# The mLSTM branch of a hybrid encoder block on one core: earlier row loads, one copy out of PSUM, the head norm in SBUF

## The chip, the core and the metric

The kernel runs on one core of a Trainium2 chip. The metric is the device time of one execution, in microseconds (us). The engines that run at the same time are PE (TensorE, matrix products), DVE (VectorE), ACT (ScalarE), POOL (GpSimd) and SP (SyncE, which here only issues DMA transfers). Each engine works its own queue in order; semaphores tie the queues together. PSUM is the memory that PE writes its products to, in banks of 512 columns; SBUF is the memory of everything else on the core.

## What is computed

One layer of a streaming encoder on 1024 tokens of width 1024: half a SwiGLU block, one projection into all the columns that a sparse attention and an mLSTM need, these two branches, their gated merge, and another half SwiGLU block. The change touches only the mLSTM branch. In the reference its scan over chunks is:

```python
D = b[..., :, None] - b[..., None, :] + ic[..., None, :]
...
W = jnp.einsum('bhtd,bhsd->bhts', qc, kc) * jnp.exp(D - m_t[..., None])
w_int = jnp.exp(inter - m_t)
num = jnp.einsum('bhts,bhsv->bhtv', W, vc) + w_int[..., None] * jnp.einsum('bhtd,bhdv->bhtv', qc, C)
den = jnp.sum(W, axis=-1) + w_int * jnp.einsum('bhtd,bhd->bht', qc, n)
h = num / jnp.maximum(jnp.abs(den), jnp.exp(-m_t))[..., None]
...
C_new = wc[..., None, None] * C + jnp.einsum('bhs,bhsd,bhsv->bhdv', ws, kc, vc)
...
h = rms_norm(h, head_g.reshape(H, MLSTM_V_DIM))
```

There are 4 heads of 64 key and 128 value columns. All of it is float32.

## The kernel before

The chip's work in this stretch is the input projection (called mixing here): each product of a 128-column block of weights is made of three float32 passes over halves of split weights, at lines 795, 796 and 797. `pump` (line 1305) advances that projection by one step, a tick, of six matmuls of 128x512, and at each tick also runs what is due: `later(n, f)` puts a function n ticks ahead, and `turn_later(n, src, then)` does the same with four PE transposes in front. ACT line 534 and POOL line 535 split each weight tile into a rounded part and its rest (`round<-raw`) ahead of the matmuls that use it. Results of the projection leave their banks through ACT lines 1230 and 1239 and DVE lines 1232, 1266 and 1271. At the same time the top-k search of the sparse attention runs in the background: counts on DVE (lines 1610 to 1617) and on ACT (lines 1640 to 1642).

`mlstm` (line 1808) handles the 1024 tokens in 8 chunks of 128 (t = 0 to 7), spread over 62 ticks, so 7.75 ticks to a chunk: half of them before the chunk's output products and half behind.

- `load(t)` fetches q, k and v of a chunk, two chunks ahead.
- `begin(t)` transposes k (line 1843) and forms k·q for the four heads (line 1846) in PSUM, and then loads two rows of 512 numbers, each broadcast to 128 partitions (line 1854): d_m into E and d_w into qw. ACT takes the exponential of E, head by head (line 1857); POOL cuts E to the causal triangle (line 1859); DVE multiplies E by k·q (line 1863) and qw by q (line 1864).
- The chunk's output is made at lines 1877 and 1878: for each head 129 columns, 128 of the numerator and one of the denominator, in banks 4 and 5 (`out`). The state is advanced by lines 1883 (PE) and 1886 (DVE).
- Then comes the head norm: DVE copies the denominators out of PSUM (line 1894) and makes reciprocals (1895 to 1897); ACT squares the four heads straight out of PSUM with row sums (line 1900); DVE line 801 and POOL line 802 take the inverse root of the means; DVE line 1903 joins both factors and line 1904 multiplies the numerators, reading PSUM. Only when line 1904 is done may the next chunk's line 1877 write banks 4 and 5.
- Seven ticks after the chunk's second half the result is transposed (line 1349), copied by ACT (line 1914) and stored to d_h (line 1915).

What order these instructions take on each engine is set by the framework's scheduler, which plans all of them by a cost model; `issue_after` puts an instruction behind another that is named. SBUF buffers are drawn from pools whose tiles the traces name extra, more, spare, plain and rawx; a DMA into a reused tile waits until its last user is done.

Of the kernel before, what the change touches and what calls it, by code (L numbers as in the profile page):

```python
# [22 lines left out]
AF = mybir.ActivationFunctionType  # L23
ALU = mybir.AluOpType
# [4 lines left out]
P = 128  # L29
# [679 lines left out]
class Block:  # L709
# [1098 lines left out]
    def mlstm(self, upto):  # L1808

        nc, ar = self.nc, self.ar  # L1810
# [15 lines left out]
        four = lambda ap: ap.rearrange("p (x e) -> p x e", x=2)  # L1826
# [10 lines left out]
        def begin(t):  # L1837
# [10 lines left out]
            kws, E, qw = ar.alloc(256), ar.alloc(512), ar.alloc(512)  # L1848
# [4 lines left out]
            for dst, src in ((E, self.d_m), (qw, self.d_w)):  # L1853
                nc.sync.dma_start(dst.f, src[t:t + 1, :].partition_broadcast(P)[:, 0, :])
# [14 lines left out]
        now = begin(0)  # L1869
        for t in range(8):  # L1870
            self.pump(halves / 8 * 0.5)
# [21 lines left out]
            den, ss = sm[t % 2].f[:, 0:4], sm[t % 2].f[:, 4:8]  # L1893
            v.tensor_copy(four(ss), out[:, :, :, 128])
            v.scalar_tensor_tensor(den, ss, -1.0, ss, ALU.mult, ALU.max)
            v.tensor_tensor(den, den, self.floor[:, t * 4:t * 4 + 4], ALU.max)
            v.reciprocal(den, den)
            nd = ar.alloc(512)
            for h in range(4):
                nc.scalar.activation(nd.f[:, h * P:(h + 1) * P], out[:, h // 2, h % 2, 0:128], AF.Square,  # L1900
                                     scale=den[:, h:h + 1], accum_out=ss[:, h:h + 1])
            self.rsqrt_mean(ss, 128, 4)
            v.tensor_tensor(den, den, ss, ALU.mult)
            v.tensor_tensor(nd.f.rearrange("p (x e c) -> p x e c", x=2, e=2), out[:, :, :, 0:128],
                            four(den)[:, :, :, None].to_broadcast([P, 2, 2, P]), ALU.mult)
            if t < 7:
                now = begin(t + 1)
            self.pump(halves / 8 * 0.5)


            def store(ps, nd=nd, t=t):
                nd.free()
                s = ar.alloc(512)
                nc.scalar.activation(s.f, ps, AF.Copy)
                nc.sync.dma_start(self.d_h[:, :, t * P:(t + 1) * P].rearrange("h p c -> p h c"),
                                  s.f.rearrange("p (h c) -> p h c", h=4))
                s.free()
# [544 lines left out]
```

## Time and profile before

| | us |
|---|---|
| median of 3 runs (lowest to highest) | 2093.31 (2091.74 to 2093.69) |
| the profiled execution | 2092.13 |
| its span in the trace | 2090.4 |
| mLSTM chunks in the trace | about 900 to 1090 |

The profiled execution lies 1.2 us under the median. Its mean granted TensorE clock is 0.997 of full speed. In a row of the timeline, what stands in brackets is the time that the engine had been idle before that instruction and what ended the idle time. Start times count from the start of the span.

### The profile page before, as it was taken

To read this page: it belongs to the slowest core of one execution; us is meant where nothing else is said; L and a number is where in the kernel's file an instruction comes from. 1 tells how busy PE (TensorE), PEld (TensorE's weight loads), DVE (VectorE), ACT (ScalarE), POOL (GpSimd) and SP (SyncE) were. 2 spreads that over 40 slices of the span, in tenths; PEclk is the share of its full clock that TensorE was granted. 3 is DMA by queue.
4 is the path that set the end of the run, shared out by engine and by line. 5 is a ranking of instruction groups with operands and counts; after the bars stand their busy time and mean duration, and the time that the engine had idled before them with its cause. 6 is when DMAs were issued, how large, how long until landed. Compare 5 with 4: busy or idle time off the path is not lost.

```text
span 2090.4 us, 27895 instructions
## 1 busy us (share of the span) xinstructions
PE 2031.9 (97%) x9341; PEld 1667.7 (80%) x9341; DVE 1615.8 (77%) x2815; ACT 1047.4 (50%) x1961; POOL 348.7 (17%) x385
## 2 busy tenths in 40 slices
PE   7999999999999989999998999999999999999999
PEld 6788888888887777787886788788888888888887
DVE  7988887678856676997899589798976676669863
ACT  8332333334436566985786478636533333334442
POOL 1000000000004223443545445312000000000000
PEclk9999999999999999999999999999999999999999
DMA  5498894494634263465665911832333333386331
GB/s 187 142 286 269 279 291 157 136 359 139 210 144 142 63 184 101 107 188 177 183 207 189 332 61 61 293 121 97 126 121 101 111 100 102 110 294 246 126 111 41
DMA packets 289677, 349.85 MB, mean 167 GB/s; under 512 B 21901, under 2 KB 187389, under 8 KB 289405
## 3 DMA queue, kind: packets, MB, share of 16 engines
q1 hardware_dynamic: 289532, 348.07, 51.1%
q8 instruction: 73, 1.20, 0.2%
q14 instruction: 72, 0.58, 0.1%
HBM read 237.34 MB, written 110.66 MB: 166 GB/s over the span
## 4 chain that ended last, share of the span: by engine, by line
PE 47%; DVE 7%; DMA 4%; ACT 3%; issue 2%; POOL 1%; SPq 0%; POOLq 0%; DVEq 0%; ACTq 0%
PE psum L795 14%; PE psum L796 14%; PE psum L797 14%; DVE plain L1610 2%; PE psum L2118 1%; PE psum L1499 1%; PE psum L1500 1%; POOL round L535 1%; PE psum L2173 1%; PE psum L2172 1%; DMA raw<-in_w_proj_b_dram 1%; DMA more<-d_m 1%; DMA side<-d_kg 0%; DVE h L925 0%; DVE plain L1529 0%
## 5 line engine op out<-in xcount | busy, mean ns | idle before, releaser
L795 PE MATMUL psum<-h,round 128*128 128x512 f32 x656 | 260.9, 398 | 3.1 <-ACT more L1239 1.5
L796 PE MATMUL psum<-h,round 128*128 128x512 f32 x656 | 258.6, 394 | 1.0 <-DVE h L925 0.8
L797 PE MATMUL psum<-h,round 128*128 128x512 f32 x656 | 258.0, 394 | 0.5 <-DVE round L302 0.3
L535 POOL TENSOR_TENSOR round<-raw,round 128x512 fp32r<-128x512 f32 x104 | 147.6, 1425 | 142.9 <-ACT round L534 109.7
L795 PEld LDWEIGHTS psum<-h,round 128*128 128x128 f32 x656 | 124.0, 189 | 31.0 <-ACT more L1239 1.9
L797 PEld LDWEIGHTS psum<-h,round 128*128 128x128 f32 x656 | 124.0, 189 | 27.4 <-DVE round L302 0.7
L796 PEld LDWEIGHTS psum<-h,round 128*128 128x128 f32 x656 | 124.2, 189 | 27.0 <-DVE h L925 1.5
L795 PE MATMUL psum<-swap,round 128*128 128x512 f32 x328 | 130.3, 398 | 7.9 <-ACT round L534 3.2
L797 PE MATMUL psum<-swap,round 128*128 128x512 f32 x328 | 129.5, 395 | 0.4 <-POOL round L535 0.4
L796 PE MATMUL psum<-swap,round 128*128 128x512 f32 x328 | 129.0, 393 | 0.4 <-DVE swap L952 0.2
L1610 DVE TENSOR_SCALAR_CACHE_REDUCE plain<-plain 128x384 bf16<-128x384 f32 (+1 forms) x124 | 107.7, 868 | 2.3
L301 ACT ACTIVATE round<-plain 128x512 fp32r<-128x512 f32 x79 | 49.6, 632 | 98.9 <-PE psum L796 77.2
L924 ACT ACTIVATE round<-plain 128x512 fp32r<-128x512 f32 x73 | 45.7, 631 | 100.0 <-PE psum L796 92.7
L878 POOL MEMSET raw<- 128x384 f32 x1 | 0.4, 422 | 526.3 <-DVE round L925 526.3
L797 PE MATMUL psum<-h,extra 128*128 128x512 f32 x212 | 82.5, 390 | 1.5 <-POOL extra L535 1.5
L796 PE MATMUL psum<-side 128*128 128x512 f32 x208 | 80.9, 389 | 0.0
L797 PE MATMUL psum<-side 128*128 128x512 f32 x208 | 80.9, 389 | 0.0
L795 PE MATMUL psum<-side 128*128 128x512 f32 x208 | 80.9, 389 | 0.0
L795 PEld LDWEIGHTS psum<-swap,round 128*128 128x128 f32 x328 | 62.0, 189 | 23.3 <-ACT round L534 4.1
L796 PE MATMUL psum<-h,spare 128*128 128x512 f32 x196 | 76.6, 391 | 1.9 <-DVE h L925 1.9
L795 PE MATMUL psum<-h,spare 128*128 128x512 f32 x196 | 76.9, 394 | 0.8 <-ACT h L924 0.4
L534 ACT ACTIVATE round<-raw 128x512 fp32r<-128x512 f32 x107 | 66.3, 624 | 21.8 <-PE psum L796 15.7
(752 smaller groups left out, 5919.9 us busy)
## 6 DMA issues: line engine op xcount, KB each, us to landing
plain<-d_a SPq DMA_DIRECT2D x154, 256.0 KB
d_a<-plain SPq DMA_DIRECT2D x123, 256.0 KB
raw<-in_ffn_w_gate_dram SPq DMA_DIRECT2D x44, 512.0 KB
raw<-d_s SPq DMA_DIRECT2D x72, 256.0 KB
h<-in_ffn_w_down_dram SPq DMA_DIRECT2D x66, 256.0 KB
plain<-in_w_in_dram SPq DMA_DIRECT2D x29, 512.0 KB
d_s<-plain SPq DMA_DIRECT2D x58, 256.0 KB
raw<-in_w_in_dram SPq DMA_DIRECT2D x55, 256.0 KB
```

The source lines that it names most:

```text
L301: k.nc.scalar.activation(hi.r.rearrange("p (k c) -> p k c", k=4), src, AF.Copy)
L534: self.done_A = k.nc.scalar.activation(hi.r, raw.f, AF.Copy).ins
L535: k.nc.gpsimd.tensor_tensor(lo.r, raw.f, hi.f, ALU.subtract)
L795: mm(ps, lhs[0], rhs[0], start=start, stop=False, skip_group_check=more)
L796: mm(ps, lhs[0], rhs[1], start=False, stop=False, skip_group_check=more)
L797: mm(ps, lhs[1], rhs[0], start=False, stop=stop, skip_group_check=more)
L924: self.split_A = self.nc.scalar.activation(hi, src, AF.Copy).ins
L1499: self.nc.tensor.matmul(o, qb, khi.r[:, s * n:s * n + n], start=True, stop=False)
L1500: last = self.nc.tensor.matmul(o, qb, klo.r[:, s * n:s * n + n], start=False, stop=True).ins
L1610: v.tensor_scalar(s.junk[:, :s.width[j]], s.sc[j], one(s.cand, j), one(s.neg, j), ALU.is_ge, ALU.add, accum_out=one(s.cnt, j))
L2118: self.last = nc.tensor.transpose(ps[:, j * P:(j + 1) * P], pr[j].f[:, kt * P:(kt + 1) * P], self.ident).ins
L2172: mm(po, vr[:, kt, g, :], hi.r, start=kt == 0, stop=False)
```

## The change

Three things are done. First, the two row loads (E and qw) leave `begin` and become a function `weights(t)`, called for the next chunk at the top of the loop, ahead of the first half of the ticks; the new chunk's `begin` is handed the two tiles. Second, one ACT copy takes all 516 columns of `out` from PSUM to an SBUF tile `nd`, behind the last weight split that ACT was given; the separate DVE copy of the denominators goes. Third, the head norm reads `nd` in SBUF, in a function `normed` that is put one tick later; its four Squares write one 128-column tile in turn, its multiplication works in place, and its transposes are put seven ticks behind it.

```diff
--- before.py
+++ after.py
@@ -1823,7 +1823,6 @@
         C = [ar.alloc(2 * 129, keep=True) for _ in range(2)]
         v.memset(C[0].f, 0.0)
         out = self.bank(4, 2).rearrange("p (x c) -> p x c", x=2)[:, :, 0:258].rearrange("p x (e c) -> p x e c", e=2)
-        four = lambda ap: ap.rearrange("p (x e) -> p x e", x=2)
 
         def load(t):
             q4 = qs[t % 2].f.rearrange("p (x e c) -> p x e c", x=2, e=2)
@@ -1834,7 +1833,14 @@
                               self.d_k[t].rearrange("x p c -> p x c"))
             nc.sync.dma_start(vs[t % 2].f.rearrange("p (h c) -> p h c", h=4)[:, :, 0:128], self.d_v[t])
 
-        def begin(t):
+        def weights(t):
+
+            E, qw = ar.alloc(512), ar.alloc(512)
+            for dst, src in ((E, self.d_m), (qw, self.d_w)):
+                nc.sync.dma_start(dst.f, src[t:t + 1, :].partition_broadcast(P)[:, 0, :])
+            return E, qw
+
+        def begin(t, E, qw):
 
             q, k = qs[t % 2].f, ks[t % 2].f
 
@@ -1845,13 +1851,11 @@
             for h in range(4):
                 mm(kq[:, h * P:(h + 1) * P], k[:, h // 2 * P:h // 2 * P + P], q[:, h * P:(h + 1) * P],
                    start=True, stop=True)
-            kws, E, qw = ar.alloc(256), ar.alloc(512), ar.alloc(512)
+            kws = ar.alloc(256)
             v.tensor_tensor(kws.f.rearrange("p (h d) -> p h d", h=4),
                             ps[:, 0:256].rearrange("p (h d) -> p h d", h=4),
                             self.ws[:, t * 4:t * 4 + 4, None].to_broadcast([P, 4, 64]), ALU.mult)
 
-            for dst, src in ((E, self.d_m), (qw, self.d_w)):
-                nc.sync.dma_start(dst.f, src[t:t + 1, :].partition_broadcast(P)[:, 0, :])
             for h in range(4):
                 r = t * 4 + h
                 nc.scalar.activation(E.f[:, h * P:(h + 1) * P], E.f[:, h * P:(h + 1) * P], AF.Exp,
@@ -1866,8 +1870,9 @@
 
         load(0)
         load(1)
-        now = begin(0)
+        now = begin(0, *weights(0))
         for t in range(8):
+            ahead = weights(t + 1) if t < 7 else None
             self.pump(halves / 8 * 0.5)
             kws, E, qw = now
             v1 = vs[t % 2].f.rearrange("p (h c) -> p h c", h=4)
@@ -1890,33 +1895,43 @@
             if t < 6:
                 load(t + 2)
 
-            den, ss = sm[t % 2].f[:, 0:4], sm[t % 2].f[:, 4:8]
-            v.tensor_copy(four(ss), out[:, :, :, 128])
-            v.scalar_tensor_tensor(den, ss, -1.0, ss, ALU.mult, ALU.max)
-            v.tensor_tensor(den, den, self.floor[:, t * 4:t * 4 + 4], ALU.max)
-            v.reciprocal(den, den)
-            nd = ar.alloc(512)
-            for h in range(4):
-                nc.scalar.activation(nd.f[:, h * P:(h + 1) * P], out[:, h // 2, h % 2, 0:128], AF.Square,
-                                     scale=den[:, h:h + 1], accum_out=ss[:, h:h + 1])
-            self.rsqrt_mean(ss, 128, 4)
-            v.tensor_tensor(den, den, ss, ALU.mult)
-            v.tensor_tensor(nd.f.rearrange("p (x e c) -> p x e c", x=2, e=2), out[:, :, :, 0:128],
-                            four(den)[:, :, :, None].to_broadcast([P, 2, 2, P]), ALU.mult)
+            nd = ar.alloc(4 * 129)
+            nd4 = nd.f.rearrange("p (x e c) -> p x e c", x=2, e=2)
+            with self.tc.issue_after(self.mp.done_A):
+                nc.scalar.activation(nd4, out, AF.Copy)
+
+
+            def normed(t=t, nd=nd, nd4=nd4, den=sm[t % 2].f[:, 0:4], ss=sm[t % 2].f[:, 4:8]):
+                sq = ar.alloc(128)
+                h4 = nd.f.rearrange("p (h c) -> p h c", h=4)
+                v.scalar_tensor_tensor(den[:, :, None], h4[:, :, 128:129], -1.0, h4[:, :, 128:129], ALU.mult, ALU.max)
+                v.tensor_tensor(den, den, self.floor[:, t * 4:t * 4 + 4], ALU.max)
+                v.reciprocal(den, den)
+                with self.tc.issue_after(self.mp.done_A):
+                    for h in range(4):
+                        nc.scalar.activation(sq.f, h4[:, h, 0:128], AF.Square,
+                                             scale=den[:, h:h + 1], accum_out=ss[:, h:h + 1])
+                sq.free()
+                self.rsqrt_mean(ss, 128, 4)
+                v.tensor_tensor(den, den, ss, ALU.mult)
+                v.tensor_tensor(h4[:, :, 0:128], h4[:, :, 0:128],
+                                den[:, :, None].to_broadcast([P, 4, 128]), ALU.mult)
+
+
+                def store(ps):
+                    nd.free()
+                    s = ar.alloc(512)
+                    nc.scalar.activation(s.f, ps, AF.Copy)
+                    nc.sync.dma_start(self.d_h[:, :, t * P:(t + 1) * P].rearrange("h p c -> p h c"),
+                                      s.f.rearrange("p (h c) -> p h c", h=4))
+                    s.free()
+
+                self.turn_later(7, lambda i: h4[:, i, 0:128], store)
+
+            self.later(1, normed)
             if t < 7:
-                now = begin(t + 1)
+                now = begin(t + 1, *ahead)
             self.pump(halves / 8 * 0.5)
-
-
-            def store(ps, nd=nd, t=t):
-                nd.free()
-                s = ar.alloc(512)
-                nc.scalar.activation(s.f, ps, AF.Copy)
-                nc.sync.dma_start(self.d_h[:, :, t * P:(t + 1) * P].rearrange("h p c -> p h c"),
-                                  s.f.rearrange("p (h c) -> p h c", h=4))
-                s.free()
-
-            self.turn_later(7, lambda i, nd=nd: nd.f[:, i * P:(i + 1) * P], store)
         for b in (*qs, *ks, *vs, *sm, *C, self.gt):
             b.free()
```

Lines 1840, 1849, 1852, 1867, 1868, 1882, 1883, 1888 and 1891 of the new kernel are lines 1854, 1843, 1846, 1863, 1864, 1877, 1878, 1883 and 1886 of the old.

SP, about 948 to 960 us of the trace, in the kernel before: `d_s` and `in_w_in` rows fetch weights, `d_kn` and `d_vs` rows store the attention's keys and values, `L1854` rows are the row loads; `more<-d_m` at row 443 belongs to chunk 2.

```order
437 L513 DMA raw<-d_s 128x512
438 L1854 DMA extra<-d_w 128x512
439 L513 DMA raw<-d_s 128x512
440 L2031 DMA d_vs<-more 128x512
441 L1980 DMA d_kn<-extra 128x512
442 L2031 DMA d_vs<-more 128x512
443 L1854 DMA more<-d_m 128x512
```

The same place after; `extra<-d_m` at row 440 belongs to chunk 3, and chunk 2's stands eight rows further up.

```order
436 L1840 DMA spare<-d_w 128x512
437 L1995 DMA d_kn<-extra 128x512
438 L1832 DMA plain<-d_k 128x2x128
439 L513 DMA raw<-d_s 128x512 x2
440 L1840 DMA extra<-d_m 128x512
441 L2046 DMA d_vs<-extra 128x512 x2
442 L1995 DMA d_kn<-extra 128x512
```

The d_m load moved ahead of the d_vs stores, and it is now that of the chunk after.

PE, the output products of chunk 3, before (`h` and `swap` are the projection's activations, `headsel` and `ident` belong to norm sums and transposes of the attention):

```order
4044 L1349 MATMUL psum<-ident,more 128x128 x4
4045 L2047 MATMUL psum<-headsel,more 128x2 x4
4046 L797 MATMUL psum<-h_4729,round 128x512
4047 L795 MATMUL psum<-h_4729,round 128x512
4048 L796 MATMUL psum<-h_4729,round 128x512
4049 L797 MATMUL psum<-h_4729,round 128x512
4050 L1877 MATMUL psum<-rawx,spare 128x129
4051 L1878 MATMUL psum<-more 128x129
```

The same place after; chunk 2's last output product is at row 3970, as against 3984 in the kernel before.

```order
3984 L796 MATMUL psum<-h_4729,round 128x512
3985 L797 MATMUL psum<-h_4729,round 128x512
3986 L1852 MATMUL psum<-plain 128x128 x4
3987 L2062 MATMUL psum<-headsel,spare 128x2 x4
3988 L795 MATMUL psum<-h_4729,round 128x512
3989 L796 MATMUL psum<-h_4729,round 128x512
3990 L1882 MATMUL psum<-rawx,extra 128x129
3991 L1883 MATMUL psum<-more,extra 128x129
```

Between the output products of chunks 2 and 3 there were 65 rows, and now there are 19; k·q of chunk 3 (row 3986, earlier row 4012) now stands four rows ahead of them.

DVE, ahead of E times k·q for chunk 2 (line 1863), before:

```order
1116 L1886 SCALAR_TENSOR_TENSOR rawx<-more,plain,psum 128x129 x2
1117 L1610 TENSOR_SCALAR plain<-plain 128x640
1118 L1903 TENSOR_TENSOR plain<-plain 128x4
1119 L1610 TENSOR_SCALAR plain<-plain 128x768
1120 L1904 TENSOR_TENSOR more<-psum,plain 128x512
1121 L1271 TENSOR_TENSOR extra<-extra,psum 128x512
1122 L1612 TENSOR_SCALAR plain<-plain 128x4
1123 L1863 TENSOR_TENSOR more<-more,psum 128x512
```

DVE, ahead of E times k·q for chunk 3 (line 1867 at row 1127), after:

```order
1117 L1610 TENSOR_SCALAR plain<-plain 128x640
1118 L1868 TENSOR_TENSOR extra<-extra,plain 128x512
1119 L2045 TENSOR_TENSOR more<-psum,more 128x4x64
1120 L1916 TENSOR_TENSOR plain<-plain 128x4
1121 L1610 TENSOR_SCALAR plain<-plain 128x768
1122 L1917 TENSOR_TENSOR more<-more,plain 128x4x128
1123 L1891 SCALAR_TENSOR_TENSOR more<-rawx,plain,psum 128x129 x2
1124 L1612 TENSOR_SCALAR plain<-plain 128x4
1125 L1481 TENSOR_TENSOR more<-spare,round 128x512
1126 L1615 SCALAR_TENSOR_TENSOR plain<-plain 128x4
1127 L1867 TENSOR_TENSOR extra<-extra,psum 128x512
```

Between qw times q (row 1118) and E times k·q (row 1127) of one chunk there now stand the norm of chunk 1 (1916, 1917), the state of chunk 2 (1891) and work of other parts.

SP, the row loads of chunk 7, before (`d_sa` rows store the top-k's result, `d_h` rows the mLSTM's):

```order
499 L518 DMA raw<-in_w_in_dram 128x4x128
500 L1915 DMA d_h<-extra 128x4x128
501 L513 DMA raw<-d_s 128x512
502 L1373 DMA d_sa<-extra 128x512
503 L518 DMA raw<-in_w_in_dram 128x4x128
504 L1854 DMA more<-d_m 128x512
505 L1854 DMA plain<-d_w 128x512
```

The same place after:

```order
499 L1840 DMA plain<-d_w 128x512
500 L1373 DMA d_sa<-spare 128x512
501 L1925 DMA d_h<-plain 128x4x128
502 L518 DMA raw<-in_w_in_dram 128x4x128
503 L1834 DMA rawx<-d_v 128x4x128
504 L1840 DMA plain<-d_m 128x512
```

Chunk 7's d_m load keeps its row 504, and its tile is now the one (plain) whose d_h store stands three rows ahead; d_w moved from row 505 to 499.

## Rows read from the trace of the kernel before

**Rows 1.** Page: PE's busy time, share and instructions among the engines; chain by engine.
```profile
PE 2031.9 (97%) x9341; PEld 1667.7 (80%) x9341; DVE 1615.8 (77%) x2815; ACT 1047.4 (50%) x1961; POOL 348.7 (17%) x385
...
PE 47%; DVE 7%; DMA 4%; ACT 3%; issue 2%; POOL 1%; SPq 0%; POOLq 0%; DVEq 0%; ACTq 0%
```

**Rows 2.** Timeline, PE: start, duration, instruction, idle time before and what ended it.
```profile
965.35 0.50 PE L795 MATMUL psum<-swap,round 128*128 128x512 f32 x1 [3.25 <-ACT round L534]
...
994.31 0.49 PE L1877 MATMUL psum<-rawx,spare 128*128 128x129 f32 x2 [2.10 <-DVE spare L1904]
...
1010.36 0.49 PE L1877 MATMUL psum<-plain,extra 128*128 128x129 f32 x2 [0.36 <-DVE extra L1904]
...
1043.36 0.46 PE L1877 MATMUL psum<-plain,extra 128*128 128x129 f32 x2 [0.68 <-ACT plain L1640]
...
1074.00 0.66 PE L1349 MATMUL psum<-ident,extra 128*128 128x128 f32 x4 [0.47 <-DVE extra L1904]
```

**Rows 3.** Windows: length, then busy of PE, PEld, DVE, ACT, POOL; PEclk; DMA share.
```profile
965.00:966.00 1.00, 0.65 (x2) 0.30 (x2) 0.47 (x1) 1.00 (x3) 0.49 (x1) 0.91 0.00 0
966.00:968.00 2.00, 1.89 (x5) 1.40 (x5) 0.29 (x2) 0.89 (x2) 0.00 (x0) 0.50 0.55 155
968.00:970.00 2.00, 2.00 (x7) 1.58 (x7) 0.69 (x1) 0.63 (x1) 0.40 (x1) 0.69 0.75 249
```

**Rows 4.** Timeline, SP: issue of transfers ahead of the stop at 965.
```profile
950.75 0.32 SPq L513 DMA_DIRECT2D raw<-d_s  x1
...
955.87 0.32 SPq L2031 DMA_DIRECT2D d_vs<-more  x1
...
960.05 0.32 SPq L1854 DMA_DIRECT2D more<-d_m  x1
...
965.80 0.38 SPq L1915 DMA_DIRECT2D d_h<-spare  x1
```

**Rows 5.** Timeline, ACT: exponentials of chunk 2, the split behind, exponentials of chunk 7.
```profile
963.50 1.28 ACT L1857 ACTIVATE more<-more,plain 128x128 f32<-128x128 f32 x4 [3.78 <-DMA more<-d_m]
964.69 0.61 ACT L534 ACTIVATE round<-raw 128x512 fp32r<-128x512 f32 x1
...
1040.47 1.28 ACT L1857 ACTIVATE more<-more,plain 128x128 f32<-128x128 f32 x4 [3.15 <-DMA more<-d_m]
```

**Rows 6.** Lines 1894 to 1857 by form: count, ns lowest/median/highest, first and last start.
```profile
L1894 DVE COPY plain<-psum x8: 149/155/159, 939.6 to 1064.5; 128x4 f32<-128x4 f32 x8
...
L1904 DVE TENSOR_TENSOR spare<-psum,plain x3: 677/686/691, 993.6 to 1042.0; 128x512 f32<-128x512 f32 x3
...
L1900 ACT ACTIVATE spare<-psum,plain x12: 343/352/370, 983.3 to 1036.9; 128x128 f32<-128x128 f32 x12
...
L1900 ACT ACTIVATION_READ_ACCUMULATOR spare<-psum,plain x12: 186/194/212, 983.6 to 1037.1; 128x1 f32 x12
...
L1914 ACT ACTIVATE spare<-psum x3: 570/597/606, 965.2 to 1060.2; 128x512 f32<-128x512 f32 x3
...
L1857 ACT ACTIVATE extra<-extra,plain x12: 384/388/404, 907.2 to 1027.9; 128x128 f32<-128x128 f32 x12
```

**Rows 7.** Timeline, DVE: a search pass, and two waits for row loads.
```profile
994.17 1.06 DVE L1610 TENSOR_SCALAR_CACHE_REDUCE plain<-plain 128x768 bf16<-128x768 f32 x1
...
995.97 0.69 DVE L1864 TENSOR_TENSOR more<-more,plain 128x512 f32<-128x512 f32 x1 [0.43 <-DMA more<-d_w]
...
1041.17 0.69 DVE L1864 TENSOR_TENSOR plain<-plain 128x512 f32<-128x512 f32 x1 [3.66 <-DMA plain<-d_w]
```

**Rows 8.** Windows: the end of the mLSTM, and the stretch behind it.
```profile
1050.00:1090.00 40.00, 39.40 (x191) 32.36 (x190) 39.26 (x95) 32.84 (x83) 16.99 (x14) 1.00 0.62 183
1100.00:1145.00 45.00, 38.27 (x169) 30.36 (x168) 43.52 (x52) 26.58 (x50) 24.12 (x15) 1.00 0.53 160
```

**Rows 9.** Timeline, PE: two waits behind the mLSTM.
```profile
1117.20 0.47 PE L795 MATMUL psum<-swap,round 128*128 128x512 f32 x1 [2.87 <-DVE plain L1266]
...
1128.76 0.50 PE L795 MATMUL psum<-side,round 128*128 128x512 f32 x1 [1.35 <-DVE more L1232]
```

## The prediction

> **What bounds the kernel now.** I read the page first: PE is busy for 2031.9 of 2090.4 us, and the chain that ended last runs through PE for 47% and through DVE for 7% [rows 1]. So there is little to win overall, and it has to come out of PE's idle time in the mLSTM stretch, about 900 to 1090 us. I then read PE's timeline there, for the brackets. They are few. One stop stands out, 3.25 us at 965.35, put down to ACT's weight split. Three of 2.10, 0.36 and 0.47 us are put down to line 1904, the multiplication that reads the output banks last, and one of 0.68 us to the search on ACT [rows 2].
>
> The stop at 965 is a chain that the other views show backwards. The split at 964.69 stood on ACT behind the four exponentials of chunk 2, and these had waited 3.78 us for the d_m row [rows 5]. That load was issued at 960.05, 4.18 us behind the d_vs store that SP had issued at 955.87 [rows 4]; in SP's order both use the tile "more", so the load had to wait until the store had landed. The chunk's row was late, and an unrelated weight split paid for it, because ACT works in order.
>
> The stop also cost clock. The windows give a granted clock of 0.91, 0.50 and 0.69 of the 2.4 GHz level in stretches of 1, 2 and 2 us behind it [rows 3], the 0.50 being the 1.2 GHz level. By those rows the loss is 0.09 x 1 + 0.50 x 2 + 0.31 x 2 = 1.7 us. So the stop is worth 3.25 + 1.7 = 4.95 us.
>
> Last, I asked what else is full. From 1050 to 1090 DVE is busy for 39.26 of 40 us beside PE's 39.40, and from 1100 to 1145 for 43.52 of 45 where PE has only 38.27 [rows 8]. There PE waits for DVE's evictions, 2.87 and 1.35 us [rows 9]. DVE is therefore the second bound, and time that PE gains early is kept only as far as DVE advances too.
>
> **Part one, the rows half a chunk earlier.** No transfer is added; 16 loads move. In SP's new order chunk 3's d_m load stands where chunk 2's stood, but ahead of the d_vs stores and behind a raw<-d_s load; the last of that kind went out at 950.75 [rows 4]. So it issues some 9 us earlier than 960.05, and the exponentials at this place on ACT find their row. The 4.95 us go. The move is not uniform: chunk 7's d_m keeps its place on SP, into the tile of a d_h store just ahead of it; chunk 5's d_m and chunk 6's d_w also wait for a d_h store. Behind chunk 7's exponentials ACT has two weight splits, so the same kind of stop can come back. Such a wait is not always paid by PE: at 1040.47 ACT waited 3.15 us for chunk 7's row [rows 5], and PE then lost only 0.68 us, to the search [rows 2]. I bound the return of that stop by 0 and 4.95 us and take 1.2, nearer to the row at 1040, where the same chunk waited.
>
> The Trainium skill bears on this part ("DMA: Bandwidth & Descriptors", Anatomy of one DMA — SWDGE (gpsimd) path): the DMA engines do not wait on semaphores, a wait is spent on the issuing sequencer before dispatch. By that, a load that moves up in the program gains nothing unless its tile and the issues ahead of it are free. The 4.18 us on SP agree; if it held for chunk 3's load as well, the 4.95 us would stay. That is one of the rivals.
>
> **Part two, one copy for the two banks.** Today the banks are held from the output products through the reciprocals, four Squares (0.35 us with a row-sum read of 0.19 each), the root and the multiplication of 0.69 us [rows 6]. After the change they are held for one ACT copy of 516 columns; the nearest row, line 1914, copies 512 from PSUM in 0.60 us [rows 6]. The three waits for line 1904 go: 2.10 + 0.36 + 0.47 = 2.93 us. The copies add 8 x 0.6 = 4.8 us to ACT, which is busy for 32.84 of 40 us at its fullest here [rows 8]; there is room, so I count none of it, but where ACT is late it adds 0.6 us.
>
> **Part three, the norm in SBUF.** DVE loses eight copies of 0.155 us [rows 6], 1.24 us. Its big multiplication gains nothing: from PSUM it takes 0.69 us [rows 6], and the SBUF one of the same size 0.69 us [rows 7]. The Squares now write one tile in turn, which no row of before shows; I bound it by 0 and half of the 0.35 us each, so 5.6 us on ACT in all, between other work, and take nothing on the path. Against reading from SBUF speaks the Trainium skill ("Perfetto Trace Analysis", Optimizing Scalar/DVE Operations): ScalarE has about 93 ns of access overhead on SBUF and 51 ns on PSUM. By it 32 Squares would cost 1.3 us more, an estimate. The trace has 0.39 us for an SBUF exponential and 0.35 for a PSUM Square of that size [rows 6], which agrees in sign.
>
> **What is late next.** Since the banks come free early, the scheduler puts chunk 3's output products 19 instructions behind chunk 2's, where it was 65, and only four rows behind their own k·q. PE therefore comes to wait for E times k·q on DVE, which has the norm of chunk 1, the state of chunk 2 and a search pass in front. If d_w is there in time, the wait is about two such DVE steps of 0.69 us less the two 512-column matmuls between: between 0.5 and 2 us, and I take 1.5. If d_w is late, it is more (a rival).
>
> **The sum.** PE's side: 4.95 + 2.93 - 1.5 - 1.2 = 5.2 us. DVE's side: it can advance by the waits for d_w that the trace shows, 3.66 and 0.43 us [rows 7], and by the 1.24 us of copies: 5.3 us. The two agree, so PE may keep its 5.2 us through the DVE-bound stretch. The profiled execution of 2092.1 us would become 2086.9; it lies 1.2 us under the median of 2093.3, so the median becomes 2088.1. A difference of about 0.2%, 4.2 us, is the least that a measurement of this kernel can tell from no change, so this is just beyond it. If part of the waits of 2.87 and 1.35 us also goes, and no new one comes, the gain is up to 7.9 + 4.2 = 12.1 us.
>
> **Rivals.**
>
> DVE gives it back. If its idle times only move (chunk 7's d_w still late, the next work not ready), DVE reaches the stretch behind 1100 earlier by the 1.24 us of copies alone, and PE's gain ends in longer waits there. For it: DVE's 43.52 of 45 us. Against it: 3.66 us of its idle time hang on one load, which moves up six rows on SP. Gain 1.2 us, 2092.1. Chance 0.17.
>
> Chunk 3's d_w is late. Its load stands on SP behind a d_h store whose counterpart went out at 965.80 [rows 4]. Then DVE stops at qw times q, and ahead of the awaited E times k·q stand four multiplications of 0.69 us, two of them those of the chunk, and a search pass of 1.06 us [rows 7]: 3.8 us, with the clock of such a stop 5.5. PE's side is 7.9 - 5.5 - 1.2 = 1.2 us, also 2092.1. Against it: without the stop at 965, that store goes out earlier too. Chance 0.12.
>
> The change does not do what it says: SP still issues the rows late, as the page's rule would have it. The 4.95 us stay, the banks' 2.93 us go, less 1.5 for chunk 3: 1.4 us, 2091.9. Chance 0.08.
>
> Slower. The three loads held by d_h stores all stop their engine: chunk 5's and chunk 7's exponentials hold weight splits (4.95 us each, as at 965), chunk 6's d_w holds DVE for 3.66 us [rows 7] in front of evictions. That is 13.6 us against 7.9 removed: 5.7 us slower, 2099.0. It decides once two of them reach PE in full beside chunk 3's wait and the third in part. For it: the new order has these waits. Against it: ACT's 3.15 us at 1040 cost PE next to nothing. Chance 0.12.
>
> **How the numbers follow.** The forecast has 0.51, with its own range from 2083.5 to 2090.5: below its centre by the waits behind 1117, above by the dearer ends of the two new waits. About 0.45 of it lies below 2089.1, that is faster by over 0.2%, the rest within. The first three rivals lie within 0.2%, but each could keep more than I priced: 0.06 of their 0.37 to faster. So faster 0.51, same 0.37, slower 0.12. The range that holds 8 in 10 starts at the forecast's lower end, 2083.5, and goes to 2096.5, where half of the slow rival lies outside.
>
> **What would show it.** Right, if the trace after has no stop of PE on line 534 around 960 with a clock of 0.5 behind it, if chunk 3's d_m is issued near 951, and if no wait for banks 4 and 5 over 0.5 us is left. The step on chunk 3 is right if PE waits 0.5 to 2 us for line 1867 there. The step on DVE is right if its waits for d_w shrink and the waits near 1117 and 1129 do not grow. Wrong, if PE's waits between 1100 and 1145 grow by what was won before, if ACT's exponentials of chunks 5 and 7 wait with a PE stop right behind, or if PE waits 3 us or more for line 1867.

## The result, and the profile after

The change makes the kernel slower: 2105.62 us median (2102.43 to 2108.05, 4 runs) beside 2092.80 us (2091.74 to 2093.69, 4 runs). The ratio is 1.0058, with a 95% interval of 1.0042 to 1.0074. 2088.1 us had been forecast.

The page after, PE's part of the line on engines:

```profile
PE 2043.4 (97%) x9341; PEld 1678.1 (80%) x9341; DVE 1612.2 (77%) x2807; ACT 1054.6 (50%) x1969; POOL 353.8 (17%) x385
```

The span grew from 2090.4 to 2104.3 us, by 13.9. PE ran the same 9341 matmuls as in [rows 1], and was busy for 11.5 us more with them. Its idle time grew by only 2.4 us, from 58.5 to 60.9. So in these two traces most of the loss is not waiting: the same matmuls took longer.

PE's timeline after shows the stops (start, duration, instruction, and in brackets the idle time before it and what ended it):

```profile
956.02 0.66 PE L1888 MATMUL psum<-rawx,more 128*64 128x129 f32 x8 [2.01 <-ACT extra L1994]
...
970.21 0.66 PE L1888 MATMUL psum<-plain,extra 128*64 128x129 f32 x8 [2.45 <-DVE more L2045]
...
990.35 0.83 PE L2062 MATMUL psum<-headsel,extra 128*128 128x2 f32 x6 [1.57 <-ACT extra L2057]
...
1004.63 0.44 PE L1849 MATMUL psum<-ident,plain 128*128 128x128 f32 x2 [1.09 <-DVE plain L2065]
...
1015.28 0.50 PE L797 MATMUL psum<-swap,round 128*128 128x512 f32 x1 [1.64 <-POOL round L535]
...
1121.34 0.76 PE L795 MATMUL psum<-swap,round 128*128 128x512 f32 x1 [2.15 <-DVE spare L1266]
...
1135.19 0.76 PE L795 MATMUL psum<-h,round 128*128 128x512 f32 x1 [3.86 <-DVE plain L1271]
...
1168.90 0.65 PE L795 MATMUL psum<-side,round 128*128 128x512 f32 x1 [3.31 <-DVE plain L1232]
```

None of the stops of [rows 2] is left: no wait for line 534 in this stretch, and none for banks 4 and 5. New ones stand in their place. Between 900 and 1090 they are smaller than the stop of 3.25 us, but four of the five shown there are followed by what followed that one. The windows behind six of the eight (the column after the five busy times is the granted clock):

```profile
955.00:960.00 5.00, 3.98 (x18) 3.10 (x19) 4.18 (x12) 2.46 (x6) 0.64 (x1) 0.75 0.47 141
970.00:975.00 5.00, 4.79 (x19) 3.74 (x20) 3.10 (x10) 1.68 (x3) 0.00 (x0) 0.66 0.58 204
990.00:995.00 5.00, 4.65 (x18) 3.83 (x19) 5.00 (x11) 3.82 (x11) 4.46 (x3) 0.66 0.86 248
1005.00:1010.00 5.00, 5.00 (x21) 4.32 (x20) 4.25 (x13) 3.79 (x11) 1.64 (x1) 0.66 0.23 70
1120.00:1125.00 5.00, 3.66 (x9) 2.98 (x10) 5.00 (x5) 0.00 (x0) 3.63 (x2) 0.66 0.03 12
1135.00:1140.00 5.00, 4.81 (x15) 3.85 (x16) 5.00 (x8) 2.73 (x5) 0.66 (x1) 0.66 0.24 74
```

A stretch of 5 us at 0.66 has lost 0.34 x 5 = 1.7 us of clock, the same as was read from [rows 3] for the stop at 965. This is one fall to 1.2 GHz and back. (The stretch at 955 shows 0.75, and the rest of that fall is in the next 5 us.) Summed over all such stretches from 880 to 1400 us, the kernel before lost 1.7 us, one fall, and the changed kernel 17.0 us, ten falls: four in 900 to 1090, three in 1100 to 1180, and three in a row at 1350 to 1360, in code that the change does not touch. Part of this lost clock covers time in which PE was idle (its busy time in the windows above is mostly under 5 us), so PE's busy time grew by 11.5 us and not by 15.3.

The two traced executions lie further apart in clock than is usual. Over the whole span the kernel before had a granted clock of 0.997 in the trace, but 0.995 in the mean of the 46 executions measured beside the experiments (0.991 to 0.998). The changed kernel had 0.990 in the trace and 0.991 in the mean of four (0.989 to 0.993). At some 2100 us, 0.001 is 2.1 us, so the means differ by about 8 us of clock, the traces by about 15. The clock is therefore a large part of the 12.8 us between the medians, but it isn't all of it: the changed kernel's one execution at 0.993 took 2105.2 us, the three of the kernel before at 0.993 took 2094.2 to 2098.5.

The two stops at the state product show how they come about. SP and ACT ahead of the one at 956, and SP and DVE ahead of the one at 970; SP first, both row loads of chunk 3:

```profile
950.31 0.32 SPq L1840 DMA_DIRECT2D extra<-d_m  x1
...
965.53 0.34 SPq L1840 DMA_DIRECT2D extra<-d_w  x1
```

ACT:

```profile
954.21 1.28 ACT L1861 ACTIVATE extra<-extra,plain 128x128 f32<-128x128 f32 x4 [0.86 <-DMA extra<-d_m]
955.39 0.57 ACT L1994 ACTIVATE extra<-psum 128x512 f32<-128x512 f32 x1
```

DVE:

```profile
969.13 0.69 DVE L1868 TENSOR_TENSOR extra<-extra,plain 128x512 f32<-128x512 f32 x1 [1.35 <-DMA extra<-d_w]
969.74 0.42 DVE L2045 TENSOR_TENSOR more<-psum,more 128x256 fp32r<-128x256 f32 x1
```

The d_m row of chunk 3 was issued at 950.31, where it was expected. But the scheduler had also put chunk 3's exponentials earlier, and they still waited 0.86 us for the row. Behind them on ACT stood line 1994, which empties one of the two PSUM banks that serve as work banks, and PE's line 1888 waited 2.01 us for that bank. At 970 the same happens on DVE: qw times q waits 1.35 us for its d_w row, issued at 965.53, and behind it stands line 2045, for which line 1888 waits 2.45 us.

The new steps cost about what had been estimated. The copy of 516 columns takes 0.58 us, against the 0.60 taken from [rows 6], and a Square into the shared tile 0.40 us, with 0.53 us from one start to the next where they follow each other directly:

```profile
L1901 ACT ACTIVATE more<-psum x4: 579/584/594, 937.8 to 1055.4; 128x516 f32<-128x516 f32 x4
```

```profile
963.07 0.40 ACT L1912 ACTIVATE rawx<-more,plain 128x128 f32<-128x128 f32 x1 [1.14 <-DVE plain L1909]
963.38 0.19 ACT L1912 ACTIVATION_READ_ACCUMULATOR rawx<-more,plain 128x1 f32 x1
963.60 0.40 ACT L1912 ACTIVATE rawx<-more,plain 128x128 f32<-128x128 f32 x1
```

### The profile page after: what moved, and what is told of

The parts are those of the page before. It is cut to its first block, busy times and chain, and to the rows that moved or that the text cites. A ratio compares the mean times of both kernels' runs of the same rounds, so it can differ in the third digit from the quotient of the medians.

```text
span 2104.3 us, 27909 instructions
## 1 busy us (share of the span) xinstructions
PE 2043.4 (97%) x9341; PEld 1678.1 (80%) x9341; DVE 1612.2 (77%) x2807; ACT 1054.6 (50%) x1969; POOL 353.8 (17%) x385
## 4 chain that ended last, share of the span: by engine, by line
PE 45%; DVE 5%; DMA 2%; ACT 1%; issue 1%; SPq 0%; POOL 0%; DVEq 0%; ACTq 0%; POOLq 0%
PE psum L795 13%; PE psum L796 13%; PE psum L797 13%; PE psum L2133 1%; PE psum L1499 1%; PE psum L1500 1%; PE psum L2188 1%; PE psum L2187 1%; DVE plain L1610 0%; DVE h L925 0%; PE psum L1852 0%; ACT h L2248 0%; DVE plain L1587 0%; PE psum L2062 0%; DMA d_aq<-round 0%
## 5 line engine op out<-in xcount | busy, mean ns | idle before, releaser
L795 PE MATMUL psum<-swap,round 128*128 128x512 f32 x328 | 132.1, 404 | 4.3 <-DVE spare L1266 2.7
L797 PE MATMUL psum<-swap,round 128*128 128x512 f32 x328 | 131.1, 400 | 1.6 <-POOL round L535 1.6
L796 PE MATMUL psum<-swap,round 128*128 128x512 f32 x328 | 130.9, 399 | 1.7 <-DVE swap L925 1.7
```

Of the source, the lines that this page charges most:

```text
L795: mm(ps, lhs[0], rhs[0], start=start, stop=False, skip_group_check=more)
L796: mm(ps, lhs[0], rhs[1], start=False, stop=False, skip_group_check=more)
L797: mm(ps, lhs[1], rhs[0], start=False, stop=stop, skip_group_check=more)
```

## The experiments

From the two traces I took theory A, that the earlier rows are the cause, by way of consumers that move up and wait in front of other work. Its rivals were B, that the early release of the banks is, and C, that any new order is. A' (A by the waits in front of other work), D, E and F came up later and are told in the expectations of the runs that tried them; E is C, with the clock as the price. In the table, the lost clock is the sum, over stretches of 5 us from 880 to 1400 us, of 5 us times what the granted clock lacks of 1; falls are that sum over 1.7 us. Times are medians. The profiled values come from one execution each; "clock" is the mean granted clock over all executions of a kernel, and a difference of one or two falls between two traces tells little.

| kernel | us | PE busy | PE idle | lost clock | falls | clock |
|---|---|---|---|---|---|---|
| before | 2092.8 | 2031.9 | 58.5 | 1.7 | 1 | 0.995 |
| after | 2105.6 | 2043.4 | 60.9 | 17.0 | 10 | 0.991 |
| e1 rows only | 2089.2 | 2036.1 | 53.1 | 8.5 | 5 | 0.995 |
| e2 norm only | 2102.5 | 2038.7 | 62.6 | 12.0 | 7 | 0.993 |
| e3 after, state product elsewhere | 2105.2 | 2042.2 | 64.5 | 15.3 | 9 | 0.991 |
| e4 before, state product elsewhere | 2098.5 | 2037.0 | 61.4 | 8.6 | 5 | 0.994 |
| e5 norm only, at once | 2109.2 | 2044.9 | 63.3 | 15.3 | 9 | 0.991 |
| e6 after, consumers held | 2111.3 | 2042.0 | 66.3 | 17.1 | 10 | 0.990 |
| e7 after, no row loads | 2095.2 | 2036.4 | 58.7 | 8.5 | 5 | 0.994 |
| e8 before, split 0.4/0.6 | 2106.2 | 2042.3 | 62.4 | 15.3 | 9 | 0.992 |
| e9 after, split 0.4/0.6 | 2111.0 | 2046.4 | 66.4 | 20.4 | 12 | 0.990 |
| e10 before, split 0.6/0.4 | 2099.6 | 2035.0 | 61.5 | 8.5 | 5 | 0.993 |
| e11 after, split 0.6/0.4 | 2100.6 | 2037.5 | 60.9 | 10.2 | 6 | 0.993 |
| e12 rows only, split 0.6/0.4 | 2109.4 | 2042.0 | 64.7 | 13.6 | 8 | 0.991 |
| e13 after, added matmuls | 2120.8 | 2059.7 | 54.8 | 8.5 | 5 | 0.993 |
| e14 before, added matmuls | 2105.7 | 2053.3 | 50.7 | 1.7 | 1 | 0.997 |

### Which part is it?

e1 keeps the first part alone, e2 the other two:

```diff
 e1, to the kernel before
+        def weights(t): ...
...
+            ahead = weights(t + 1) if t < 7 else None
...
-                now = begin(t + 1)
+                now = begin(t + 1, *ahead)
 e2, to the changed kernel
-        def weights(t): ...
...
-        def begin(t, E, qw):
+        def begin(t):
...
+            for dst, src in ((E, self.d_m), (qw, self.d_w)): ...
```

> The kernel before with the first part alone: the two row loads at the top of the loop. Theory A (the earlier rows let the scheduler put the exponentials and qw times q ahead of the copies that empty the two work banks, there they still wait 0.9 to 1.4 us for their transfers, and PE's short stops behind them drop the clock): 2100 to 2107 us, granted clock about 0.991. Theory B (the early release of banks 4 and 5 brings the chunks' output products close together, and PE then waits for the two work banks): 2086 to 2091 us, since the stop of 4.95 us at 965 goes and nothing comes. Theory C (any new order of this stretch moves PE's stops, and each short stop may cost clock): 2095 to 2101.

> The kernel before with the copy out of the two banks and the later norm in SBUF, but the row loads where they were, in begin. Theory A: 2088 to 2093 us, the waits for line 1904 gone, the clock as before. Theory B: 2100 to 2107 us, with PE waiting for the work banks at the state product and a clock of about 0.991. Theory C: 2095 to 2101.

e1 measured 2089.2 us, ratio 0.9992 (0.9981 to 1.0003): no difference. e2 measured 2102.5, ratio 1.0047 (1.0032 to 1.0062). That speaks against theory A, and C's range (2095 to 2101) was missed by both. But e1 is no plain confirmation of theory B either. Its PE timeline, and the windows behind:

```profile
970.65 0.47 PE L795 MATMUL psum<-swap,round 128*128 128x512 f32 x1 [1.05 <-DVE spare L1271]
...
972.62 0.57 PE L795 MATMUL psum<-h,round 128*128 128x512 f32 x1 [1.26 <-DVE extra L1232]
```

```profile
970.00:975.00 5.00, 3.09 (x11) 2.22 (x11) 5.00 (x10) 3.55 (x12) 2.79 (x3) 0.79 0.31 101
975.00:980.00 5.00, 5.00 (x19) 4.51 (x20) 4.00 (x19) 1.89 (x3) 2.60 (x3) 0.53 0.67 230
```

Two stops of 1.05 and 1.26 us, waits for evictions, replaced the one of 3.25 and cost 1.05 + 2.35 = 3.4 us of clock in these 10 us. In the whole kernel PE's idle time fell by 5.4 us, close to the 4.95 us priced for the stop; PE's busy time grew by 4.2 through four more falls, and it took most of that back.

In e2, the waits are not those of theory B. None of the three large ones is for a work bank at the state product; they are for a weight split on POOL, an eviction on DVE and the norm's multiplication (line 1911 in this kernel), for whose result the transposes of line 1349 wait:

```profile
980.93 0.50 PE L797 MATMUL psum<-swap,round 128*128 128x512 f32 x1 [3.39 <-POOL round L535]
...
1008.52 0.57 PE L795 MATMUL psum<-side,round 128*128 128x512 f32 x1 [3.03 <-DVE spare L1232]
...
1042.68 1.11 PE L1349 MATMUL psum<-ident,spare 128*128 128x128 f32 x4 [4.25 <-DVE spare L1911]
```

### Is it the work banks?

e3 and e4 take the state product out of the work banks, into columns 258 to 386 of banks 4 and 5, which nothing uses:

```diff
-                st = self.psB()
+                st = self.bank(4, 2).rearrange("p (x c) -> p x c", x=2)[:, :, 258:387]
...
```

> The changed kernel, with the state product (line 1888) written into columns of banks 4 and 5 that nothing uses, so that it no longer takes one of the two work banks. The two stops of PE there, 2.01 and 2.45 us, with 1.7 us of clock each, come to 7.9 us. Theories A and B: about 2098 us, and no wait of line 1888 left. Theory C: the stops move elsewhere, 2102 to 2108.

> The kernel before, with the state product in the free columns of banks 4 and 5. In the trace before no wait of line 1883 over 0.2 us stands, so theories A and B expect no change, 2090 to 2094 us. Theory C: any other order costs, 2095 to 2101.

e3 measured 2105.2 us, ratio 1.0064 (1.0049 to 1.0079), like the changed kernel. The two waits of line 1888 at 956 and 970 are gone (one of 1.32 us stands at 1007), but the stops went elsewhere, one of 3.45 us for line 534 at 988 among them. e4 measured 2098.5, ratio 1.0027 (1.0014 to 1.0040): slower, though it only frees PE from a resource. Both came out as theory C had it: a new order costs, whatever it was made for.

### Is it the later norm, or the waits for rows?

```diff
 e5, to e2
-            self.later(1, normed)
+            normed()
 e6, to the changed kernel: the four exponentials and qw times q
+                with self.tc.issue_after(self.mp.done_A):
                     nc.scalar.activation(E.f[...], ..., AF.Exp, ...)
+            with self.tc.issue_after(self.done_V):
                 v.tensor_tensor(qw.f, qw.f, q, ALU.mult)
 e7, to the changed kernel
+            r0 = ar.alloc(512, keep=True)
+            nc.sync.dma_start(r0.f, src[0:1, :]...)
...
-                nc.sync.dma_start(dst.f, src[t:t + 1, :]...)
...
```

> Row loads in begin as before, the copy out of the banks and the norm in SBUF as in the change, but the norm at once and not one tick later. Theory D (the later norm puts its DVE and ACT steps into other places, and its results come late for the transposes): 2090 to 2095 us, against 2102 with the later norm. Theory E (any order in which ACT and DVE meet waiting transfers at other places makes short stops of PE, and each takes about 1.7 us of clock besides itself; the part of the change does not matter): 2096 to 2104.

> The changed kernel, with the exponentials of E held behind the newest weight split and qw times q behind the newest eviction, so that neither stands on ACT or DVE ahead of work that PE needs soon. Theory A' (the waits of these two for their rows, in front of such work, are the cause): 2092 to 2098 us, with no PE stop behind them. Theory E: 2098 to 2108, the stops elsewhere.

> The changed kernel without the 16 row loads: one row is loaded once, and every chunk uses it for E and for qw (this part of the computation is left out). Theory A': what waits for rows is gone, 2088 to 2094 us, clock 0.996. Theory E (other waits for transfers, stores whose tiles are reused, stop ACT and DVE as well): 2096 to 2104, clock 0.99 to 0.994.

e5 measured 2109.2 us, ratio 1.0074 (1.0059 to 1.0090): with the norm at once it is slower than with the later norm, so theory D falls. e6 measured 2111.3, ratio 1.0084 (1.0068 to 1.0101), which speaks against theory A': held back, the consumers of the rows cost more. Both lie above E's ranges too (2096 to 2104 and 2098 to 2108). e7 measured 2095.2, ratio 1.0007 (0.9996 to 1.0019), 10 us under the changed kernel, with a clock of 0.994: between the ranges, 1.2 us above that of A' and 0.8 below E's. So without the loads this code runs as fast as the kernel before, but not faster, and its PE still stops for others. Its waits from 880 to 1200 (releaser, us in total, times, longest):

```profile
engine line waited for: us in total, times, longest us
PE psum L797 <- POOL round L535: 5.6, 3, 3.5
PE psum L795 <- DVE more L1271: 4.0, 1, 4.0
PE psum L795 <- DVE more L1232: 2.0, 1, 2.0
```

Since e7 also has another order, it doesn't tell how much of its 10 us is the rows themselves. That part stays open: in the changed kernel the stops at 956, 970 and 1004 do have such a wait for a row ahead of them, on ACT or DVE.

### Is it the order alone?

e8 changes nothing but the order: the share of a chunk's ticks ahead of its output products.

```diff
-            self.pump(halves / 8 * 0.5)
+            self.pump(halves / 8 * 0.4)
...
-            self.pump(halves / 8 * 0.5)
+            self.pump(halves / 8 * 0.6)
```

> The kernel before, with 0.4 of a chunk's ticks ahead of its output products and 0.6 behind (0.5 each before): no instruction is added or changed, only the order. Theories A' and D: 2089 to 2096 us. Theory E: this order too has its own short stops, 2096 to 2102, clock 0.992 to 0.995.

It measured 2106.2 us, ratio 1.0055 (1.0035 to 1.0076), with nine falls: with no instruction changed, as slow as the changed kernel, and 4 us above E's range.

One stop shows how an order makes PE wait. At 1135.19 the changed kernel's PE waits 3.86 us for line 1271, an eviction on DVE. DVE waits for nothing there; it works through two passes of the top-k selection (1587, 1589) and the squares of the keys' norm (2010) first:

```profile
1127.20 3.00 DVE L1587 TENSOR_TENSOR_SCAN plain<-more 128x896 f32<-128x896 f32 x1
1130.12 2.25 DVE L2010 TENSOR_TENSOR spare<-plain 128x1024 f32<-128x1024 f32 x1
1132.30 2.15 DVE L1589 SCALAR_TENSOR_TENSOR more<-plain,more 128x896 f32<-128x896 f32 x1
1134.37 0.68 DVE L1271 TENSOR_TENSOR plain<-plain,psum 128x512 f32<-128x512 f32 x1
```

In the kernel before, the same eviction goes ahead of the pass:

```profile
1125.52 0.68 DVE L1271 TENSOR_TENSOR plain<-plain,psum 128x512 f32<-128x512 f32 x1
1126.11 2.02 DVE L1587 TENSOR_TENSOR_SCAN spare<-plain 128x896 f32<-128x896 f32 x1
```

The stop isn't tied to the change. It stands, at 4.03 to 4.08 us, in e3, e6, e7, e9 and e13, but also in e10, which is the kernel before with another split, and in e12, which has the early rows alone; e11, which has the whole change, doesn't have it.

So the change was compared with the kernel before at two other splits, 0.4/0.6 and 0.6/0.4:

> The changed kernel with the ticks split 0.4 to 0.6 around the output products, to be set against the kernel before with the same split (2106.2 us). Theory E (the order that the scheduler lands on decides; the order of the kernel before happens to have one fall of the clock where others have 5 to 10): the change is worth little in itself, 2098 to 2108 us, on either side of 2106. Theory F (the change itself costs, in any order): 2114 to 2122.

> The kernel before with the split 0.6 to 0.4. Theory E: 2096 to 2107 us, with 5 to 10 falls of the clock (1.7 us each in the windows). Theory F: 2089 to 2097.

> The changed kernel with the split 0.6 to 0.4. Theory E: 2095 to 2108 us, within 6 us of the kernel before at this split. Theory F: 10 to 15 us over it.

> The early row loads alone, with the split 0.6 to 0.4. Theory E: 2092 to 2106 us, not tied to the 2089 us of the 0.5 split. If the early rows are worth something in any order: 3 to 6 us under the kernel before at this split.

| split | before | after | difference | rows only |
|---|---|---|---|---|
| 0.4/0.6 | 2106.2 | 2111.0 | +4.8 | |
| 0.5/0.5 | 2092.8 | 2105.6 | +12.8 | 2089.2 |
| 0.6/0.4 | 2099.6 | 2100.6 | +1.0 | 2109.4 |

At 0.6/0.4 the runs of before (2096.3 to 2102.0) and after (2099.6 to 2103.3) overlap; at 0.4/0.6 the two were measured on different chips, and their intervals against the kernel before, 1.0035 to 1.0076 and 1.0061 to 1.0099, overlap too. The early rows alone are level at one split and 9.8 us slower at another. Theory F, a cost of 10 to 15 us in any order, doesn't hold at 0.6/0.4; a smaller cost of a few us isn't excluded. Theory E has its direction confirmed, since the order alone moves the time by about 6 and 13 us, but not its sizes: e10 and e11 lie in its ranges, e9 and e12 are 3 us above, and e5, e6 and e8 were above theirs as well. It doesn't foretell what an order costs. In its trace the kernel before has the fewest falls of e1 to e12; by the clock of all executions e1 is level with it. Only e1, and e7 with its loads left out, were as fast: the order of the kernel before is near the best of those tried, so an edit that moves the order had more to lose than to gain. The change brings no gain at any of the three splits.

### Does the clock hang on what PE leaves undone?

e13 and e14 put eight matmuls of 254 columns, without use, ahead of each chunk's state product, in the changed kernel and in the kernel before:

```diff
+                for _ in range(8):
+                    mm(self.bank(4)[:, 258:512], ks[t % 2].f[:, 0:P], qs[t % 2].f[:, 0:254], start=True, stop=True)
                 st = self.psB()
```

> The changed kernel with eight matmuls of 254 columns without use ahead of each chunk's state product, into columns of bank 4 that nothing reads: by the 0.11 us of a 129-column matmul some 0.2 us each, 56 of them 12 us of PE, less what fills idle time. If the falls come from PE's idle time around its stops: at most 2 falls between 900 and 1090 us (there are 6 in the changed kernel), and 2104 to 2112 us in spite of the 12 us. If they do not hang on it: 5 or more falls, 2112 to 2120 us.

> The kernel before with the same eight matmuls per chunk. In the kernel before there is one fall in this stretch. If the falls come from PE's idle time around its stops: none or one, and 12 us minus what fills idle time: 2096 to 2105 us. If a changed order alone decides: 3 or more falls, 2106 to 2115 us.

Two numbers in these expectations were wrong: the changed kernel has four falls in that stretch, not six, and each of the added matmuls runs as two. In e14 a chunk's eight stand as 16 in one row:

```profile
953.21 3.59 PE L1881 MATMUL psum<-plain 128*128 128x254 f32 x16
```

3.59 us a chunk, and 25 us in all rather than 12. e14 measured 2105.7 us (three runs), 13.7 over the kernel before beside it, so 11 us of the 25 don't show in the time; PE's idle time is 7.8 us less. The time lies between the two ranges, which end at 2105 and begin at 2106. e13 measured 2120.8 (two runs, 2116.2 and 2125.4), above both of its ranges. Neither has a fall between 900 and 1090; behind it e13 has five, up to 1370, and e14 one. The windows of e14:

```profile
900.00:950.00 50.00, 49.45 (x251) 40.85 (x250) 40.70 (x100) 35.84 (x88) 21.10 (x20) 1.00 0.57 161
950.00:1000.00 50.00, 48.27 (x287) 40.84 (x286) 40.17 (x116) 31.40 (x82) 19.68 (x16) 1.00 0.58 182
1000.00:1050.00 50.00, 49.52 (x285) 42.29 (x285) 37.08 (x97) 32.55 (x90) 25.66 (x22) 1.00 0.57 172
1050.00:1100.00 50.00, 50.00 (x255) 42.12 (x254) 43.24 (x106) 37.78 (x93) 20.42 (x16) 1.00 0.56 167
```

The clock is at 1.00 throughout, and PE is busy for 197.2 of the 200 us. In this stretch e14 has no stop of PE over 0.73 us. So the falls hang on PE's idle time around its stops: an order costs clock by the stops that it makes. What this leaves open is that both fills are new orders as well, with one trace each; the other fourteen kernels all have at least one fall in this stretch. And idle time doesn't settle it alone: e13 keeps stops of 1.21 and 1.66 us there without a fall. As a remedy the fill doesn't pay at this size.

## Why the prediction was wrong

- **The stop at 965 goes: right.** It went in the changed kernel and in e1. The step that put chunk 3's load near 951 held to 0.7 us. That the exponentials would find their row did not: they waited 0.86 us, since they had moved up as well.
- **The waits for line 1904 go: right, with one misread.** The 2.93 us went, and the copy took 0.58 us, for 0.60. But the 0.47 us at 1074 wasn't a wait for the banks: line 1349 there transposes the norm's result, so an earlier release couldn't remove it. In e2 the same kind of wait is 4.25 us.
- **The norm in SBUF takes nothing on the path: not shown.** The size was about right. In the trace before, four Squares followed at 0.35 us from start to start, one Square's length [rows 6]; now it is 0.53 where they follow directly. If all 32 did, that would be 5.8 us on ACT, just over the upper bound of 5.6; ACT's busy time grew by 7.2 us, copies included. But e2, which has parts two and three alone, was 10 us slower than the kernel before. The Trainium skill ("Perfetto Trace Analysis", Optimizing Scalar/DVE Operations) gives ScalarE about 93 ns of access overhead on SBUF and 51 ns on PSUM, 42 ns more. The trace agrees, 0.40 for 0.35 us.
- **What is late next: wrong in place and in price.** I named one place, chunk 3's output products, and PE doesn't stop there. It stops at two state products and at the transposes of k (1004), for work banks behind ACT and DVE steps that wait for rows, and also at a norm sum (990) and for a weight split on POOL (1015). And I priced each new stop at its idle time, 1.5 and 1.2 us, though [rows 3] had shown that a stop of 3.25 us costs 1.7 us of clock besides; the upper bound of 4.95 us and two of the rivals had it in their prices, the 1.5 and the 1.2 that went into the sum had not. This is the term that failed: in place of 2.7 us, the new stops between 900 and 1090 come to 9.65 us (the five shown there and two of 0.57 and 0.32) and four falls, 6.8 us of clock. The six falls behind 1100 stood at nothing in the sum, as did any change of order there.
- **DVE's side: wrong.** Its waits for d_w were to shrink from 3.66 and 0.43 us by all of that. A third, of 1.97 us for chunk 2's row, had been overlooked, so they were 6.1 us before; after, they are 7.5 us (2.25, 1.35, 1.35 and 2.53). ACT's waits for d_m did shrink, from 13.6 to 8.8 us. Behind 1100 PE's waits, of which [rows 9] show two, are now three of 2.15, 3.86 and 3.31 us, where before there were six of at most 2.87. Their sum hardly changed; but three falls came with them.
- **The rivals.** The slower one was right in sign and wrong in mechanism: it had three held loads stop their engines for 4.95 and 3.66 us, and PE behind them. Chunk 6's d_w held DVE for 2.53 us and chunk 7's d_m held ACT for 1.37, but PE has no stop there. That d_w of chunk 3 comes late was a rival too, priced at 5.5 us; it came 1.35 us late, and PE paid 2.45 us and a fall of 1.7, at the state product.
- **The sum as a whole.** It took the order of before, with some waits removed and two added. But PE's order changed through the whole mLSTM stretch, and e8 shows that this alone, with nothing removed or added, moves the time by 13 us. A range from 2083.5 to 2096.5 was too narrow for that.

## What to carry to other kernels

Where a scheduler places the work, a small edit gives a new order of everything near it, and its effect on the time may be larger than what the edit itself saves: before crediting an edit, time a few orders that change nothing (here a split of 0.4 or 0.6), with and without it. Count a stop of TensorE at its idle time plus the clock that may fall behind it, and read the granted clock beside PE's busy time: a PE that is busier with the same matmuls has lost clock, not gained work. A load that is moved up need not end the wait for it: here what consumes it moved up too and still waited. Holding the consumers back (e6) didn't help.

## What was not expected of the hardware

Each fall of the clock cost the same, 1.7 us in the windows, behind stops of very different length: 1.09 us at 1004.63 and 3.86 us at 1135.19. But the number of falls at a stop isn't fixed. The stop for line 1271 (3.86 to 4.08 us) has one fall in the changed kernel, e7, e10 and e12, and two in e3, e6, e9 and e13. And not every stop costs one. The kernel before had stops of 2.10 and 2.87 us [rows 2, 9] whose following 5 us are at full clock:

```profile
994.00:999.00 5.00, 4.69 (x38) 4.26 (x39) 4.57 (x17) 3.70 (x10) 1.85 (x2) 1.00 0.32 82
1117.00:1122.00 5.00, 4.80 (x21) 4.03 (x22) 5.00 (x5) 0.99 (x2) 2.50 (x2) 1.00 0.36 107
```

In the changed kernel the stop of 1.64 us at 1015.28 had no fall behind it, the one of 1.57 at 990.35 had. The same pair of stops, at the same lines, goes either way. The kernel before and e14, each with 5 us right behind its pair:

```profile
1340.42 0.50 PE L795 MATMUL psum<-swap,round 128*128 128x512 f32 x1 [1.60 <-ACT swap L924]
...
1342.49 0.51 PE L795 MATMUL psum<-swap,spare 128*128 128x512 f32 x1 [1.11 <-DVE h L2236]
...
1343.00:1348.00 5.00, 4.82 (x21) 4.02 (x22) 2.86 (x8) 1.03 (x3) 0.00 (x0) 1.00 0.93 316
```

```profile
1352.75 0.50 PE L795 MATMUL psum<-swap,round 128*128 128x512 f32 x1 [1.61 <-ACT swap L924]
...
1354.81 0.49 PE L795 MATMUL psum<-swap,spare 128*128 128x512 f32 x1 [1.10 <-DVE h L2238]
...
1355.00:1360.00 5.00, 4.80 (x14) 3.57 (x14) 3.19 (x8) 1.04 (x3) 0.31 (x1) 0.66 0.84 274
```

So the length of a stop doesn't tell whether the clock falls, and what does isn't settled by these runs. The same program varies with it: the kernel before took from 2088.1 to 2099.0 us over these 46 executions, on three chips, more than the 0.2% that I had taken as the least difference to be told. The eight of them with a granted clock of 0.993 or less took 2097.4 us in the mean, the others 2092.2.
